# The remainders of the second feed-forward matrix formed by an adding DMA instead of VectorE, in a two-layer decoder trunk

## The chip, the cores and the metric

The kernel runs on one core of one Trainium2 chip. The metric is the device time of one execution in microseconds (us); lower is better.

## What is computed

The reference is a trunk of two layers on 512 tokens of width 1024, in float32. The first layer mixes with differential attention and block-sparse attention, the second with gated linear attention. Each mixer is followed by a residual, a layer norm, and a feed-forward network of 4096 hidden channels, and by another residual and norm. The change touches the feed-forward network alone:

```python
def sqrelu_mlp(x, w1, w2):
    return jnp.square(jax.nn.relu(x @ w1)) @ w2
...
x = layer_norm(DEEPNORM_ALPHA * x + mix, ln_mix_g[l], ln_mix_b[l])
x = layer_norm(DEEPNORM_ALPHA * x + sqrelu_mlp(x, ffn_w1[l], ffn_w2[l]), ln_ffn_g[l], ln_ffn_b[l])
```

## The kernel before, in words

**Split products.** Every large product is made in three passes. A float32 operand is split into a rounded part (type float32r) and a remainder, its difference from the rounded part, rounded in turn. `mm3` (L170 to L173) multiplies high by high, then the two mixed pairs. In the second feed-forward product the activations `hh` and `hl` are the stationary operands and the weights move: L171 takes the rounded part of the weight, L172 its remainder, L173 the rounded part again.

**The weight stream.** All weights lie in DRAM as units of 128x1024 float32 (512 KB), in the order in which they are used (`wst`). SP's queue loads them into a ring of four `raw` tiles (L92). `split_unit` (L114) pops one and calls `parts` (L105): ScalarE (ACT) copies it with rounding into half 0 of a `w` tile (L110), and VectorE (DVE) subtracts half 0 from `raw` and writes half 1 (L111). The `raw` tile is free again when both have read it. `w` tiles come from the pool `up` of eleven buffers; a count of slots (`W["cap"]`, 7 in the feed-forward network) limits how far ahead of their use units are split. `free` gives slots back when a unit has been used and calls `pump`, which splits the next unit.

**A feed-forward layer** (`ffn`) works in four blocks of eight hidden tiles (b = 0 to 3). In each block first the eight units of the first matrix are used, giving `hh` and `hl`, and then the eight units of the second matrix. In blocks 1 to 3 the first-matrix units are taken two at a time by `pair`, a scheme with seven products for eight, whose sums of weights `split_pair` forms on DVE (tile `sf`); block 0 uses six plain units and one pair. The products of the second matrix go to the four PSUM tiles `pf`, half a row of output at a time: four units for the first half, then four for the second. One such unit feeds 24 matmuls of 512 columns (2 slices of 128 channels, 4 token tiles, 3 passes). In the last block of each layer, POOL also loads the norm's gain and bias (`gb`, L290), by two DMAs on its own queue.

The order on each engine is set by the tile framework's scheduler, which may move an instruction ahead of others written earlier when its operands are ready. Each engine then works through its list in order.

Of the kernel before, what the change touches and what calls it, by code (L numbers as in the profile page):

```python
# [15 lines left out]
AF = mybir.ActivationFunctionType  # L16
ALU = mybir.AluOpType
AX = mybir.AxisListType

P = 128  # L20
# [4 lines left out]
FF = 4096  # L25
# [11 lines left out]
FBLK = 8  # L37
# [4 lines left out]
FFN_UNITS = (32, 128)  # L42
# [4 lines left out]
def trunk(ctx, tc, a, out):  # L47
    nc = tc.nc
    V, A, G, PE = nc.vector, nc.scalar, nc.gpsimd, nc.tensor
# [31 lines left out]
    wst = a["wst"]  # L81
# [2 lines left out]
    W = {"dma": 0, "split": 0, "used": 0, "slots": 0, "cap": 6}  # L84
    pairs = {u + 16 * b + j for u in FFN_UNITS for b in range(FF // P // FBLK) for j in range(0 if b else NPLAIN, FBLK, 2)}

    def dma_unit():
        for fn in late.pop(W["dma"], ()):
            fn()
        if W["dma"] < NU:  # L90
            r = rp.tile([P, 1024], F32, tag="raw", name="raw")
            nc.sync.dma_start(r, wst[W["dma"]])  # L92
            raws[W["dma"]] = r
            W["dma"] += 1

    def pop_raw():
        u = W["split"]
        while W["dma"] <= u:
            dma_unit()
        W["split"] += 1  # L100
        return raws.pop(u)

    def ahead():
        while W["dma"] < min(W["split"] + 4, NU):
            dma_unit()  # L105

    def parts(w, i, src):

        n = src.shape[-1] // 512
        A.activation(w[:, 0, i:i + n, :], src.rearrange("p (n c) -> p n c", n=n), AF.Copy)  # L110
        V.tensor_tensor(w[:, 1, i:i + n, :], src.rearrange("p (n c) -> p n c", n=n), w[:, 0, i:i + n, :].bitcast(F32),  # L111
                        op=ALU.subtract)

    def wtile():  # L114
        return up.tile([P, 2, 2, 512], F32R, tag="u", name="w")

    def split_unit():
        u = W["split"]
        if u in pairs:
            return split_pair(u)  # L120
        w = wtile()
        parts(w, 0, pop_raw())
        units[u] = w.rearrange("p s n c -> p s (n c)")
        W["slots"] += 1
        ahead()

    def split_pair(u):

        a1, a2 = pop_raw(), pop_raw()
        a11, a12, a21, a22 = a1[:, :512], a1[:, 512:], a2[:, :512], a2[:, 512:]  # L130
        ta, tb, tc_, td = (wtile() for _ in range(4))
        sf = t8("sf", (P, 2048))
        s1, s2, s3, s4 = (sf[:, 512 * i:512 * i + 512] for i in range(4))
        parts(ta, 0, a1)
        V.tensor_tensor(s1, a21, a22, op=ALU.add)
        V.tensor_tensor(s2, s1, a11, op=ALU.subtract)
        parts(tb, 0, sf[:, :1024])
        V.tensor_tensor(s3, a11, a21, op=ALU.subtract)
        V.tensor_tensor(s4, a12, s2, op=ALU.subtract)
        parts(tc_, 0, sf[:, 1024:])  # L140
        parts(td, 0, a22)
        units[u] = (ta, tb, tc_, td)
        W["slots"] += 4
        ahead()

    def pump():
        n = 4 if W["split"] in pairs else 1
        if W["split"] < NU and W["slots"] + n <= W["cap"]:
            split_unit()

    def nxt():
        u = W["used"]
        while W["split"] <= u:
            split_unit()
        W["used"] += 2 if u in pairs else 1
        return units.pop(u)
# [1040 lines left out]
```

## Time and profile before

| | us |
|---|---|
| median of three runs | 1173.81 |
| lowest and highest of them | 1173.73 and 1173.92 |
| the profiled execution, its own time | 1172.42 |
| its span, from first to last instruction | 1170.6 |

The profile is of one execution. It gives the busy time of each engine (PE is TensorE, PEld its weight loads), the chain of work that ended last, the waits between engines, and a timeline of instructions with start, duration and the idle time before each with what ended it. All times in it are counted from the start of the span.

### The profile page before, as it was taken

What the parts mean: (1) busy time and instruction counts of PE and PEld (TensorE: products, weight loads), DVE (VectorE), ACT (ScalarE), POOL (GpSimd) and SP (SyncE); (2) the same over time, 40 slices, a digit from 0 to 9 for tenths busy, and PEclk for the clock granted to TensorE, in tenths of its full rate; (3) what the DMA queues carried; (4) which work ended last, traced back from release to release, by engine and by line L of the source; (5) the groups of instructions that cost most, each with busy time, mean ns of one, the idle gap of its engine ahead of it and who ended that gap; (6) DMA issues with size and microseconds to landing.
All of it is one profiled execution on the core that took longest, in us unless ns stands there. A gap on an engine that the chain in (4) does not pass through costs nothing.

```text
span 1170.6 us, 16693 instructions
## 1 busy us (share of the span) xinstructions
PE 1155.2 (99%) x6682; PEld 1008.9 (86%) x6682; DVE 793.0 (68%) x1299; ACT 548.1 (47%) x890; POOL 48.4 (4%) x64
## 2 busy tenths in 40 slices
PE   9999999999999999999999999999999999999997
PEld 6788877898899899899888888888988998988986
DVE  6788673679468477487547656587784874865946
ACT  5745375547237146156236433643471551642631
POOL 1122300000000000000110000000000000000000
PEclk9999999999999999999999999999999999999999
DMA  9622050023226125127123122501051251251421
GB/s 319 232 72 73 8 161 32 19 73 118 99 60 191 38 73 180 54 67 252 37 68 108 55 72 73 180 19 57 34 181 54 70 165 55 87 165 36 121 78 73
DMA packets 34094, 114.33 MB, mean 98 GB/s; under 512 B 4192, under 2 KB 5216, under 8 KB 34016
## 3 DMA queue, kind: packets, MB, share of 16 engines
q1 hardware_dynamic: 32368, 108.22, 28.6%
q0 software_dynamic: 1648, 5.05, 1.4%
q8 instruction: 52, 0.85, 0.3%
q14 instruction: 26, 0.21, 0.1%
HBM read 111.15 MB, written 2.10 MB: 97 GB/s over the span
## 4 chain that ended last, share of the span: by engine, by line
PE 93%; issue 2%; ACT 2%; DVE 1%; DMA 0%; POOL 0%; DVEq 0%; ACTq 0%; POOLq 0%
PE pf L171 11%; PE pf L172 11%; PE pf L173 11%; PE pp L173 7%; PE pp L172 7%; PE pp L171 7%; PE pa L171 5%; PE pa L173 5%; PE pa L172 5%; PE pb L171 3%; PE pb L172 3%; PE pb L173 3%; PE pl L1000 2%; PE sc L521 1%; PE pv L171 1%
## 5 line engine op out<-in xcount | busy, mean ns | idle before, releaser
L111 DVE TENSOR_TENSOR w<-raw,w 128x1024 fp32r<-128x1024 f32 (+1 forms) x190 | 222.2, 1179 | 57.2 <-ACT w L110 56.3
L110 ACT ACTIVATE w<-raw 128x1024 fp32r<-128x1024 f32 (+1 forms) x190 | 188.2, 997 | 92.2 <-DMA raw<-in_wst 19.9
L171 PE MATMUL pf<-w,hh 128*128 128x512 f32 x504 | 196.4, 390 | 0.0
L172 PE MATMUL pf<-w,hh 128*128 128x512 f32 x504 | 196.2, 389 | 0.0
L173 PE MATMUL pf<-w,hl 128*128 128x512 f32 x504 | 196.1, 389 | 0.0
L110 ACT ACTIVATE w<-sf 128x1024 fp32r<-128x1024 f32 x52 | 55.0, 1058 | 215.6 <-PE pf L173 138.7
L172 PE MATMUL pp<-xTl,w 128*128 128x256 f32 x416 | 117.7, 283 | 0.0
L173 PE MATMUL pp<-xTh,w 128*128 128x256 f32 x416 | 117.7, 283 | 0.0
L171 PE MATMUL pp<-xTh,w 128*128 128x256 f32 x416 | 117.7, 283 | 0.0
L173 PEld LDWEIGHTS pf<-w,hl 128*128 128x128 f32 x504 | 94.6, 188 | 19.8
L171 PEld LDWEIGHTS pf<-w,hh 128*128 128x128 f32 x504 | 94.6, 188 | 19.5
L172 PEld LDWEIGHTS pf<-w,hh 128*128 128x128 f32 x504 | 94.6, 188 | 19.1
L171 PE MATMUL pa<-xTh,w 128*128 128x512 f32 x264 | 106.0, 403 | 0.0
L173 PE MATMUL pa<-xTh,w 128*128 128x512 f32 x264 | 103.1, 391 | 0.0
L172 PE MATMUL pa<-xTl,w 128*128 128x512 f32 x264 | 102.9, 390 | 0.0
L111 DVE TENSOR_TENSOR w<-sf,w 128x1024 fp32r<-128x1024 f32 x52 | 63.6, 1224 | 56.5 <-ACT w L110 56.5
L171 PE MATMUL pp<-T,w 128*128 128x256 f32 x312 | 88.3, 283 | 0.0
L172 PE MATMUL pp<-T,w 128*128 128x256 f32 x312 | 88.3, 283 | 0.0
L173 PE MATMUL pp<-T,w 128*128 128x256 f32 x312 | 88.3, 283 | 0.0
L171 PEld LDWEIGHTS pp<-xTh,w 128*128 128x128 f32 x416 | 79.8, 192 | 0.3
L172 PEld LDWEIGHTS pp<-xTl,w 128*128 128x128 f32 x416 | 79.8, 192 | 0.3
L173 PEld LDWEIGHTS pp<-xTh,w 128*128 128x128 f32 x416 | 79.8, 192 | 0.0
(260 smaller groups left out, 2264.2 us busy)
## 6 DMA issues: line engine op xcount, KB each, us to landing
raw<-in_wst SPq DMA_DIRECT2D x190, 512.0 KB, 3.8
xraw<-in_xT SPq DMA_DIRECT2D x8, 256.0 KB, 5.1
x<-in_x SPq DMA_DIRECT2D x4, 512.0 KB, 6.9
gb<-in_lng POOLq DMA_DIRECT2D x4, 512.0 KB, 5.7
gb<-in_lnb POOLq DMA_DIRECT2D x4, 512.0 KB, 7.5
out_x<-x SPq DMA_DIRECT2D x7, 256.0 KB, 2.0
tab<-in_rope SPq DMA_DIRECT2D x2, 512.0 KB, 5.9
raw<-in_wst SPq DMA_DIRECT2D x4, 128.0 KB, 4.4
```

The source lines that it names most:

```text
L110: A.activation(w[:, 0, i:i + n, :], src.rearrange("p (n c) -> p n c", n=n), AF.Copy)
L111: V.tensor_tensor(w[:, 1, i:i + n, :], src.rearrange("p (n c) -> p n c", n=n), w[:, 0, i:i + n, :].bitcast(F32), op=ALU.subtract)
L171: PE.matmul(o, l[0], r[0], start=first, stop=False)
L172: PE.matmul(o, l[0], r[1], start=False, stop=False)
L173: PE.matmul(o, l[1], r[0], start=False, stop=last)
L521: PE.matmul(ps[:, :n], q, k, start=i == 0, stop=False)
L1000: PE.matmul(pl[:, h * P:(h + 1) * P], z, z, start=True, stop=True)
```

## The change

For the 64 units of the second feed-forward matrix (eight in each of four blocks of two layers) DVE's subtraction is gone. ACT reads `raw` a second time and writes the negated rounded part into half 1 of the `w` tile. Then a DMA on POOL's queue reads the same unit again from DRAM and adds it to half 1. All other units, and the units of the first matrix, are split as before.

```diff
+    second = {u + 16 * b + 8 + j for u in FFN_UNITS for b in range(FF // P // FBLK) for j in range(FBLK)}
+
...
         w = wtile()
-        parts(w, 0, pop_raw())
+        raw = pop_raw()
+        if u in second:
+            A.activation(w[:, 0], raw.rearrange("p (n c) -> p n c", n=2), AF.Copy)
+            A.activation(w[:, 1], raw.rearrange("p (n c) -> p n c", n=2), AF.Copy, scale=-1.0)
+            nc.gpsimd.dma_start(w[:, 1], wst[u].rearrange("p (n c) -> p n c", n=2), accum_op=ALU.add)
+        else:
+            parts(w, 0, raw)
         units[u] = w.rearrange("p s n c -> p s (n c)")
```

In the changed kernel the lines behind the new code stand eight further down (`parts` is L112 and L113, the two new copies are L126 and L127, the DMA is L128, `p1` is L780). PE's list is the same in both, instruction for instruction.

ACT, block 0 of the first layer, from the last part of the pair's weights to the fifth second-matrix unit (`w_2627` is the block's first such unit; `r` and `hh` are the hidden activations, `p1` a partial sum of the pair). Before:

```order
L110 ACTIVATE w_2577<-raw_2443 128x512
L110 ACTIVATE w_2627<-raw_2479 128x1024
L707 ACTIVATE r_2657<-pa_2632 128x512
L110 ACTIVATE w_2664<-raw_2515 128x1024
L712 ACTIVATE r_2657<-r_2657 128x512
L110 ACTIVATE w_2704<-raw_2591 128x1024
L714 ACTIVATE hh_2660<-r_2657 128x512
L772 ACTIVATE p1_2675<-pp_2671 128x256
L110 ACTIVATE w_2736<-raw_2593 128x1024
L110 ACTIVATE w_2779<-raw_2630 128x1024
```

The same place in the changed kernel:

```order
L112 ACTIVATE w_2577<-raw_2443 128x512
L126 ACTIVATE w_2627<-raw_2479 128x1024
L127 ACTIVATE w_2627<-raw_2479 128x1024
L715 ACTIVATE r_2658<-pa_2633 128x512
L126 ACTIVATE w_2665<-raw_2515 128x1024
L720 ACTIVATE r_2658<-r_2658 128x512
L127 ACTIVATE w_2665<-raw_2515 128x1024
L722 ACTIVATE hh_2661<-r_2658 128x512
L126 ACTIVATE w_2706<-raw_2591 128x1024
L127 ACTIVATE w_2706<-raw_2591 128x1024
L780 ACTIVATE p1_2677<-pp_2673 128x256
L126 ACTIVATE w_2739<-raw_2593 128x1024
```

The second copy of the first unit stands right behind the first copy; the later units and `p1` stand one to three copies further back than they did.

POOL, last block of the first layer (`w_4973` is its first second-matrix unit). Before, these three stood next to each other:

```order
L290 DMA gb_5138<-in_lng 128x1024
L290 DMA gb_5138<-in_lnb 128x1024
L849 DMA wgr_5518<-in_wg 128x128
```

In the changed kernel:

```order
L128 DMA w_4973<-in_wst 128x1024
L128 DMA w_5017<-in_wst 128x1024
L128 DMA w_5070<-in_wst 128x1024
L298 DMA gb_5167<-in_lng 128x1024
L128 DMA w_5103<-in_wst 128x1024
L128 DMA w_5147<-in_wst 128x1024
L298 DMA gb_5167<-in_lnb 128x1024
L128 DMA w_5198<-in_wst 128x1024
L128 DMA w_5228<-in_wst 128x1024
L128 DMA w_5258<-in_wst 128x1024
L857 DMA wgr_5550<-in_wg 128x128
```

The block's eight adding DMAs stand around the two loads of `gb`; five of them come behind the first of these.

## Rows read from the trace of the kernel before

**Rows 1.** The page: span, busy time and share of each engine.
```profile
span 1170.6 us, 16693 instructions
PE 1155.2 (99%) x6682; PEld 1008.9 (86%) x6682; DVE 793.0 (68%) x1299; ACT 548.1 (47%) x890; POOL 48.4 (4%) x64
```

**Rows 2.** The page: the chain that ended last, shares of the span by engine.
```profile
PE 93%; issue 2%; ACT 2%; DVE 1%; DMA 0%; POOL 0%; DVEq 0%; ACTq 0%; POOLq 0%
```

**Rows 3.** PE's waits, all of 254 to 590 us, then all of 830 to 1162.
```profile
PE pf L171 <- ACT xTh L338: 0.3, 1, 0.3
...
PE pf L171 <- ACT xTh L338: 0.2, 1, 0.2
```

**Rows 4.** DVE's groups by line and form, 254 to 1170: idle before at the end.
```profile
L111 DVE TENSOR_TENSOR w<-raw,w 128x1024 fp32r<-128x1024 f32 x128 | 155.0, 1222 | 38.2 <-ACT w L110 37.7
```

**Rows 5.** Timeline of ACT: start, duration, instruction. Block 0, first unit and the pair's `hh`.
```profile
280.08 1.04 ACT L110 ACTIVATE w<-raw 128x1024 fp32r<-128x1024 f32 x1
281.03 0.58 ACT L707 ACTIVATE r<-pa 128x512 f32<-128x512 f32 x1
...
295.61 0.61 ACT L714 ACTIVATE hh<-r 128x512 fp32r<-128x512 f32 x1
```

**Rows 6.** Timeline of PE: the first unit's first uses, block 0, then the fourth unit's.
```profile
290.00 0.40 PE L171 MATMUL pf<-w,hh 128*128 128x512 f32 x1
290.24 0.40 PE L172 MATMUL pf<-w,hh 128*128 128x512 f32 x1
...
306.35 0.39 PE L171 MATMUL pf<-w,hh 128*128 128x512 f32 x1
```

**Rows 7.** Timeline, block 1: ACT's first copy, PE's first remainder, ACT's last `hh`.
```profile
359.66 1.06 ACT L110 ACTIVATE w<-raw 128x1024 fp32r<-128x1024 f32 x1 [0.35 <-PE pp L173]
360.63 0.37 ACT L772 ACTIVATE p<-pp 128x256 f32<-128x256 f32 x1
...
374.10 0.40 PE L172 MATMUL pf<-w,hh 128*128 128x512 f32 x1
...
377.40 1.14 ACT L714 ACTIVATE hh<-r 128x512 fp32r<-128x512 f32 x2
```

**Rows 8.** The page, DMA queues (packets, MB, share of 16 engines) and issues (median landing).
```profile
q1 hardware_dynamic: 32368, 108.22, 28.6%
q0 software_dynamic: 1648, 5.05, 1.4%
...
raw<-in_wst SPq DMA_DIRECT2D x190, 512.0 KB, 3.8
gb<-in_lng POOLq DMA_DIRECT2D x4, 512.0 KB, 5.7
gb<-in_lnb POOLq DMA_DIRECT2D x4, 512.0 KB, 7.5
```

**Rows 9.** Tile `gb`, landings of its two DMAs at 144, 536, 735 and 1113.
```profile
DMA to landing us min/median/max: 3.7/4.4/5.0
DMA to landing us min/median/max: 6.6/7.4/8.1
DMA to landing us min/median/max: 5.3/6.7/8.0
DMA to landing us min/median/max: 6.0/6.5/6.9
```

**Rows 10.** Busy time by stretch: PE, PEld, DVE, ACT, POOL, clock, DMA share, GB/s.
```profile
283.00:290.00 7.00, 7.00 (x60) 7.00 (x59) 6.60 (x10) 4.60 (x7) 0.00 (x0) 1.00 0.93 311
360.00:375.00 15.00, 15.00 (x122) 14.81 (x122) 14.27 (x22) 11.46 (x16) 0.00 (x0) 1.00 0.74 234
536.00:544.00 8.00, 8.00 (x59) 7.59 (x59) 7.73 (x12) 4.65 (x6) 1.04 (x2) 1.00 0.84 303
```

**Rows 11.** Timeline of POOL in the last block of the first layer.
```profile
536.28 0.53 POOL L290 DMA_DIRECT2D gb<-in_lng  x1 [390.94 <-PE pp L173]
```

**Rows 12.** Timeline of ACT, the last block's first second-matrix copy.
```profile
527.38 1.06 ACT L110 ACTIVATE w<-raw 128x1024 fp32r<-128x1024 f32 x1 [0.35 <-PE pp L173]
```

## The prediction, made before the changed kernel ran

> **What bounds the kernel.** I read the page's busy times first, then the chain, then PE's own waits in the two stretches of feed-forward work, and only then the engines that the change touches. PE is busy for 1155.2 of 1170.6 us [rows 1]; the reader is to see that 15.4 us is all that could be won without changing a matmul. The chain that ended last is PE for 93% and DVE for 1% [rows 2]. In the two feed-forward stretches PE waits once each for another engine, 0.3 and 0.2 us, both times for ACT's transposed input and never for a weight [rows 3]. So DVE, although it is busy for 793.0 us, is not what PE waits for here. What matters is the other question: how early each remainder is ready now, and whether the new path is still in time.
>
> **What goes from DVE.** The subtraction of 64 units, at 1222 ns each [rows 4]: 64 x 1.222 = 78.2 us, of 793.0. I cost the gain at nothing, since no PE wait in the stretch ends on DVE [rows 3]. Were all of PE's waits there gone, it would be 0.5 us.
>
> **What comes to ACT.** A second copy of the same shape for 64 units. A copy follows another at 281.03 - 280.08 = 0.95 us [rows 5], so 64 x 0.95 = 61 us on top of 548.1, on an engine that is 47% busy [rows 1]. What hides it is ACT's idle time, and behind that the lead of `hh`. In block 1 (and alike in 2 and 3) the last pair's `hh` end at 377.40 + 1.14 = 378.5 and the fourth unit uses them: 373.86 is where the first unit starts, 0.24 before its remainder at 374.10 [rows 7], and units follow at (306.35 - 290.00) / 3 = 5.45 us [rows 6], so that is 390.2. The lead is 11.7 us. ACT's new list puts twelve copies of second-matrix units ahead of this `hh` where eight stood: 4 x 0.95 = 3.8 us, still hidden if ACT's idle time (3.5 us of the 15 from 360 to 375 [rows 10]) took none of it. In block 0 the pair's `hh` ends at 296.2 and is used at 306.35 [rows 5, 6], a lead of 10.1 us. If that cover were gone, each further microsecond of ACT would be one of PE.
>
> **What comes to POOL and the DMA engines: the first unit.** After the second copy POOL issues a DMA of 512 KB, and PE's L172 waits for it. Its time is not in this trace; plain DMAs on the same queue and of the same size are. Below: the shortest of them, 3.7 us from issue to landing [rows 9]. Above: an addition has to read what is in SBUF as well as what is in DRAM, so it can move as much as two transfers. The nearest row for that is the second of the two `gb` loads, which lands when both are through: 5.0 to 8.1 us, median 7.5 [rows 8, 9]. In busy stretches even a first load took up to 6.6, and two more transfers' worth of engine time on top of it (1.70 each, below) make 10.0, my upper end. I take 7.5, because the DMA engines are 93% busy in the stretch that decides [rows 10], nearer to the rows at 536 than to those at 144.
>
> In block 0 the first unit's copy starts at 280.08; the second copy starts at 281.03 and ends at about 282.1 [rows 5]. The remainder is first read at 290.24 [rows 6], 8.1 us later. With 7.5 it lands at 289.6, 0.6 us early; with 3.7 it is 4.4 us early; with 8.1 it is just in time; with 10.0 it is 1.9 us late. The second layer's block 0 is built alike, so the upper end is 2 x 1.9 = 3.8 us. In blocks 1 to 3 the first copy ends at 360.7, `p` goes between, and the second ends at about 362.0 [rows 7]; the remainder is read at 374.10, 12.1 us later. All of 3.7 to 10.0 fits.
>
> **The later units.** PE takes one every 5.45 us, so a queue that delivers faster never falls behind. Plain transfers cost, in time of all 16 engines: 28.6% of 1170.6 us for 108.22 MB, or 1.62 us for one unit on SP's queue; 1.4% for 5.05 MB, or 1.70 us for one on POOL's [rows 8]. An adding transfer lies between 1.70 (one) and 3.40 (two). Beside it, while units are split in a burst, one `raw` load each has to pass: 3.3 to 5.0 us for both. Both ends are under 5.45, so the first unit is the only one that is tight, and I cost the others at nothing. The cover is 0.4 us per unit at the upper end, and more when the `raw` loads pause. The Trainium skill, "Collectives: The Full Stack", section "The bandwidth ceiling: the fold count and why AG ≠ RS ≠ AR", speaks against this change: a DMA that adds has two sources to read through one read ring and so moves data at half the rate of a copy. By that rule the transfer would cost an estimated 3.40 us and the sum would be the same, 0, with 0.4 us of cover per unit; at a copy's rate the cover would be 2.1 us. No run here shows yet which holds.
>
> **POOL's queue.** Issuing one DMA took 0.53 us [rows 11], eight in a block 4.2, against 43.6 us of matmuls for them (8 x 5.45). In the last block of a layer the loads of `gb` stand among them, and the first waited for PE until 536.28 [rows 11]; five adding DMAs now stand behind it, the fourth unit's first. That block's burst of copies begins at 527.38 [rows 12], so by block 1's distances (374.10 - 359.66 [rows 7], then 3 x 5.45) the fourth remainder is read at 558.2, 21.9 us after `gb` got its buffer. I cost this at nothing.
>
> **The sum.** 0 from DVE, 0 from ACT, 0 from the later units, 0 from the first unit with bounds 0 and 3.8. The profiled execution's own 1172.4 us stays 1172.4, and the runs' median, 1.4 us above it, stays **1173.8 us**.
>
> **The rivals.**
> - *Adding is dear in sustained rate (slower).* The place is the second matrix of all eight blocks, the point from which it decides 5.45 us of engine time for one adding transfer, 3.2 plain ones. At four plain ones (6.8 us) and even with no `raw` load beside them, the eighth of a block lands at 362.0 + 2 + 8 x 6.8 = 418.4 (2 us for what a landing of 3.7 holds beside 1.70 of transfer), and its use is 374.1 + 7 x 5.45 = 412.2: 6.2 us late, times 8 blocks 50 us, 1223 us; eight `raw` loads beside them, 8 x 1.62 = 13 us a block, could bring it to 1327. For it: no row shows an adding transfer or one that writes float32r. Against: plain transfers leave a factor of three. Chance 0.18.
> - *The first unit alone is late (a little slower).* Landings from 9.3 us on cost over 1.2 us in each layer, over 0.2% in all; 10.0 us gives 1177.6. For it: the busy DMA engines in that stretch [rows 10]. Against: the changed list frees `raw` tiles later for the second and third unit, so the loads beside it thin out. Chance 0.14.
> - *POOL cannot launch while DVE works (slower).* If DVE's instructions held back POOL's making of a DMA, the first unit of block 0 would be launched only in a gap of DVE, which is busy for 6.60 of the 7 us to 290 [rows 10]; launched then and landing 3.7 to 8.1 us later it is about 5 us late in each layer, 1184. The row against it: at 536.28 a DMA was issued in 0.53 us, and both landed by 8.1, in a stretch with DVE busy for 7.73 of 8 [rows 9 to 11]. The Trainium skill, "SBUF — State Buffer", has the rule in its note "The 'DVE blocks DMA' trap": DVE's two-port modes, such as a float32 copy, lock GpSimd out of writing descriptors. DVE's work here is tensor-tensor, for which the note does not claim that; the trace agrees as far as it goes. Chance 0.03.
> - *PE gains (faster).* DVE loses a tenth of its work, and anything that it held up would come earlier. PE's waits of 0.5 us are the ceiling: 1173.3, within the same. More would need faster matmuls, and the granted clock is already 1.00 of 2.4 GHz in every stretch shown [rows 10]. Chance 0.03.
>
> **How the numbers follow.** A measurement of this kernel can tell about 0.2% (2.35 us) from no change. No change to that bound: 0.62. Slower by more: 0.18 + 0.14 + 0.03 = 0.35. Faster by more: 0.03. The likeliest case alone runs from 1173.3 to 1176.2. The range reaches on to the cases of a late first unit and of a held launch, up to 1185; below, 1172.3 leaves room for a slight gain. Left out are the dear transfers, 0.18, and a real gain.
>
> **What would show it.** In the new profile PE's waits in 254 to 590 us should hold nothing for `w`, or only the L172 right behind the first L171 of block 0, around 290 and 867, by under 2 us. POOL's 64 DMAs should land in 5 to 10 us; DVE should be near 715 us, ACT near 609. The landings of one block should come closer together than 5.45 us. I am wrong if PE waits for `w` in blocks 1 to 3, with waits that grow from unit to unit: then the adding transfer is dear. I am also wrong if the landing is short and PE still waits: then ACT's second copy or POOL's queue is late.

## The result, and the profile after

The change makes the kernel slower: 1180.3 us median (1178.68 to 1181.48, four runs) against 1173.77, a ratio of 1.0055 with a 95% interval of 1.0038 to 1.0073. I had forecast 1173.8 us as the likeliest, with a chance of 0.35 for slower; the time lies inside the range but not in the case that I called likeliest.

The profiled execution took 1181.48 us. Its page, the lines that answer to [rows 1, 8]:

```profile
span 1179.7 us, 16801 instructions
...
PE 1159.7 (98%) x6682; PEld 1012.0 (86%) x6682; DVE 721.7 (61%) x1235; ACT 605.3 (51%) x954; POOL 104.2 (9%) x128
...
q1 hardware_dynamic: 32368, 108.22, 27.3%
q0 software_dynamic: 10864, 38.61, 15.8%
...
raw<-in_wst SPq DMA_DIRECT2D x190, 512.0 KB, 4.6
w<-in_wst POOLq DMA_DIRECT2D x64, 512.0 KB, 12.1
```

DVE lost 71.3 us and ACT gained 57.2, near the 78 and 61 that I had costed. The adding DMAs land in 12.1 us at the median, where I took 7.5 for the first of a block and had said 5 to 10 for all 64; by tile (`w` on POOL) their spread is

```profile
DMA to landing us min/median/max: 7.8/12.1/20.0
```

PE's waits in the same profile (in all, times, longest), all of them of 1 us or more and those of the feed-forward stretches:

```profile
PE pf L180 <- DMA w<-in_wst: 4.9, 4, 2.1
PE pn L601 <- ACT sh L596: 2.2, 1, 2.2
PE pt L536 <- ACT k L462: 1.8, 1, 1.8
PE idle L78 <- DVE zero L75: 1.2, 1, 1.2
PE p L179 <- ACT xTh L249: 1.1, 1, 1.1
PE pf L179 <- ACT xTh L346: 0.8, 3, 0.3
```

The first line is new. The reader is to see that 60 of 64 adding DMAs made PE wait for nothing, and four did. The timeline of PE shows which (start, duration, instruction, idle before and what ended it); L180 is the pass that reads the remainder:

```profile
293.80 0.50 PE L180 MATMUL pf<-w,hh 128*128 128x512 f32 x1 [1.98 <-DMA w<-in_wst]
...
570.49 0.50 PE L180 MATMUL pf<-w,hh 128*128 128x512 f32 x1 [0.31 <-DMA w<-in_wst]
...
574.28 0.50 PE L180 MATMUL pf<-w,hh 128*128 128x512 f32 x1 [2.14 <-DMA w<-in_wst]
575.54 0.60 PE L179 MATMUL pf<-w,hh 128*128 128x512 f32 x1
575.94 0.63 PE L180 MATMUL pf<-w,hh 128*128 128x512 f32 x1
...
578.93 0.43 PE L181 MATMUL pf<-w,hl 128*128 128x512 f32 x1
...
876.38 0.50 PE L180 MATMUL pf<-w,hh 128*128 128x512 f32 x1 [0.45 <-DMA w<-in_wst]
```

Two are the first unit of block 0, one in each layer (293.80 and 876.38). The other two are the seventh and eighth unit of the first layer's *last* block (570.49 and 574.28), a place where I had seen no danger. Behind the longest wait the matmuls take 0.63 us instead of 0.39. The table of stretches (PE, PEld, DVE, ACT, POOL, granted clock, DMA share, GB/s) shows the granted clock there, and at a place in the attention part:

```profile
176.00:180.00 4.00, 4.00 (x16) 3.47 (x16) 1.25 (x3) 3.07 (x7) 0.00 (x0) 0.57 0.50 161
...
576.00:579.00 3.00, 3.00 (x9) 2.35 (x8) 2.50 (x9) 1.74 (x4) 0.00 (x0) 0.50 0.00 0
579.00:582.00 3.00, 3.00 (x15) 2.47 (x14) 1.69 (x4) 0.00 (x0) 0.00 (x0) 1.00 0.00 0
```

From 576 to 579 the granted clock is 0.50, the lower level of 1.2 GHz; the eight steps from 575.54 to 578.93 take 3.39 us, where eight of 5.45 / 24 take 1.82, 1.6 us more. So the span's 9.1 us more are 4.9 us of waits for `w` and 4.5 us of longer busy time (1159.7 less 1155.2), with 0.3 us less of other idle time. Of the 4.5 us the stretch behind the last block's wait makes up 1.6, and the one at 176 us, which lies ahead of every adding DMA, an estimated 1.7 (4 us at 0.57). This execution was the slowest of the four; the median lies 1.2 us lower.

### The profile page after: what moved, and what is told of

Same layout as the page of the kernel before. It is cut to its first block, busy times and chain, and to the rows that moved or that the text cites. A ratio compares the mean times of both kernels' runs of the same rounds, so it can differ in the third digit from the quotient of the medians.

```text
span 1179.7 us, 16801 instructions
## 1 busy us (share of the span) xinstructions
PE 1159.7 (98%) x6682; PEld 1012.0 (86%) x6682; DVE 721.7 (61%) x1235; ACT 605.3 (51%) x954; POOL 104.2 (9%) x128
## 3 DMA queue, kind: packets, MB, share of 16 engines
q0 software_dynamic: 10864, 38.61, 15.8%
## 4 chain that ended last, share of the span: by engine, by line
PE 89%; DMA 4%; ACT 3%; issue 2%; DVE 1%; POOL 0%; SPq 0%; DVEq 0%; POOLq 0%; ACTq 0%
PE pf L180 11%; PE pf L179 10%; PE pf L181 10%; PE pp L181 6%; PE pp L180 6%; PE pp L179 6%; PE pa L179 5%; PE pa L181 5%; PE pa L180 5%; PE pb L179 4%; PE pb L180 4%; PE pb L181 4%; DMA w<-in_wst 3%; PE pl L1008 2%; PE sc L529 1%
## 5 line engine op out<-in xcount | busy, mean ns | idle before, releaser
L180 PE MATMUL pf<-w,hh 128*128 128x512 f32 x504 | 197.5, 392 | 4.9 <-DMA w<-in_wst 4.9
L113 DVE TENSOR_TENSOR w<-raw,w 128x1024 fp32r<-128x1024 f32 x126 | 144.9, 1156 | 76.3 <-ACT w L112 75.7
L112 ACT ACTIVATE w<-raw 128x1024 fp32r<-128x1024 f32 x126 | 120.7, 967 | 77.1 <-DMA raw<-in_wst 24.6
L112 ACT ACTIVATE w<-sf 128x1024 fp32r<-128x1024 f32 x52 | 55.0, 1058 | 176.6 <-PE pf L181 58.8
L128 POOL DMA_DIRECT2D w<-in_wst x64 | 55.9, 873 | 744.4 <-ACT w L127 724.5
L180 PE MATMUL pp<-xTl,w 128*128 128x256 f32 x416 | 117.8, 283 | 0.0
L180 PEld LDWEIGHTS pf<-w,hh 128*128 128x128 f32 x504 | 95.1, 189 | 25.7 <-DMA w<-in_wst 6.4
L180 PE MATMUL pa<-xTl,w 128*128 128x512 f32 x264 | 103.0, 390 | 0.0
L723 DVE TENSOR_TENSOR hl<-r,hh 128x512 fp32r<-128x512 f32 x64 | 44.2, 690 | 73.1 <-ACT hh L722 72.8
L180 PE MATMUL pp<-T,w 128*128 128x256 f32 x312 | 88.4, 283 | 0.0
L113 DVE TENSOR_TENSOR w<-sf,w 128x1024 fp32r<-128x1024 f32 x52 | 63.6, 1222 | 34.1 <-ACT w L112 34.1
L179 PEld LDWEIGHTS pp<-xTh,w 128*128 128x128 f32 x416 | 79.9, 192 | 0.3
## 6 DMA issues: line engine op xcount, KB each, us to landing
w<-in_wst POOLq DMA_DIRECT2D x64, 512.0 KB, 12.1
```

The source lines that it names most:

```text
L128: nc.gpsimd.dma_start(w[:, 1], wst[u].rearrange("p (n c) -> p n c", n=2), accum_op=ALU.add)
L179: PE.matmul(o, l[0], r[0], start=first, stop=False)
L180: PE.matmul(o, l[0], r[1], start=False, stop=False)
L723: V.tensor_tensor(l, r, h.bitcast(F32), op=ALU.subtract)
```

## The experiments

**Where the loss sits.** Theory A: only where an adding DMA is longer than the lead of its unit. Theory B: a small loss at each of the 64 units. Three kernels put the new path into parts of the network, a fourth takes it out at the late places:

```diff
-    second = {u + 16 * b + 8 + j for u in FFN_UNITS for b in range(FF // P // FBLK) for j in range(FBLK)}
+    second = {u + 16 * b + 8 + j for u in FFN_UNITS for b in (1, 2) for j in range(FBLK)}      # e1
+    second = {u + 8 + j for u in FFN_UNITS for j in range(FBLK)}                               # e2
+    second = {FFN_UNITS[0] + 48 + 8 + j for j in range(FBLK)}                                  # e3, e10
...
+    second -= {u + 8 for u in FFN_UNITS} | {FFN_UNITS[0] + 56 + j for j in range(4, FBLK)}     # e4, behind the line of the change
```

> The adding DMA only in blocks 1 and 2 of both layers (32 of 64 units); the other units are split on DVE as before. Theory A (late places): PE waits only for the first unit of block 0 and the last units of the last block, because only there an adding DMA of 8 to 20 us is longer than the lead; then this kernel has no PE wait for w and takes 1173.8 us within 0.2%. Theory B (every unit costs): the loss is spread over the units by the doubled DMA traffic and ACT's second copies, 6.5 us / 64 each; then it takes 1173.8 + 3.3 = 1177.0 us.

> The adding DMA only in block 0 of both layers (16 units). Theory A: PE waits for the first unit of block 0 as in the changed kernel, 2.1 us in the first layer and about 0.6 in the second, 1176.5 us, and up to 1.6 us more where a wait drops the granted clock. Theory B: 16 units, 1175.4 us, without a single long wait.

> The adding DMA only in the last block of the first layer (8 units). Theory A: the seventh and eighth unit are late as in the changed kernel, 2.6 us of waits and 1.6 us of lower clock behind them, 1176.4 to 1178.0 us. Theory B: 8 units, 1174.6 us.

> The whole change, but the late units stay on DVE: the first unit of block 0 in both layers and the last four units of the first layer's last block (6 of 64). Theory A: no PE wait for w is left, 1173.8 us within 0.2%. Theory B: 58 units still cost 5.9 us, 1179.7 us.

| kernel | units by DMA | median us | before, same chip | ratio, 95% interval | PE's waits for `w` in the profile |
|---|---|---|---|---|---|
| e1, blocks 1 and 2 | 32 | 1173.9 | 1173.12 | 1.0006 [0.9996, 1.0016] | none |
| e2, block 0 | 16 | 1175.99 | 1173.12 | 1.0017 [1.0006, 1.0028] | 1.9 us, 2 times |
| e3, last block, layer 1 of 2 | 8 | 1178.26 | 1173.12 | 1.0040 [1.0024, 1.0055] | 2.5 us, 2 times |
| e4, all but six | 58 | 1172.38 | 1173.12 | 0.9997 [0.9986, 1.0009] | none |

The ratio is worked out from all runs of both kernels, so it is not exactly the quotient of the two medians.

Theory B falls: 32 units cost nothing, 58 units cost nothing, and eight at the wrong place cost 0.4%. The losses of e2 and e3 add up to 0.57%, against 0.55% for the whole change. In e4 the 58 adding DMAs still take 11.8 us to land at the median; the page of e4 and PE's waits in its two feed-forward stretches read as those of before [rows 1, 3]:

```profile
PE 1155.8 (99%) x6682; PEld 1009.9 (86%) x6682; DVE 729.4 (62%) x1241; ACT 599.8 (51%) x948; POOL 99.3 (8%) x122
```
```profile
PE pf L180 <- ACT xTh L347: 0.3, 1, 0.3
...
PE pf L180 <- ACT xTh L347: 0.2, 1, 0.2
```

**What the parts cost by themselves.** e5 leaves the DMA out, e6 lets it copy instead of add:

```diff
-            nc.gpsimd.dma_start(w[:, 1], wst[u].rearrange("p (n c) -> p n c", n=2), accum_op=ALU.add)    # e5
+            nc.gpsimd.dma_start(w[:, 1], wst[u].rearrange("p (n c) -> p n c", n=2))                      # e6, in its place
```

> The DMA is left out: half 1 keeps the negated rounded part, so the remainders are not formed; DVE's 64 subtractions stay away and ACT's 64 second copies stay. Theory A: DVE's relief is worth nothing and ACT's copies are hidden, 1173.8 us within 0.2%. Rival (ACT's second copies cost): slower than before by more than 0.2%. Rival (DVE's relief gains): faster by more than 0.2%.

> The DMA copies the unit over half 1 instead of adding it (the remainders are replaced by the rounded weights); same queue, same size, same waits. Theory A (adding moves two operands): landings come 1.7 to 2.0 us apart in a burst instead of 3.8, the first lands in about 6 us instead of 8 to 10, PE waits for w nowhere, 1173.8 us within 0.2%. Rival (the cast to float32r or POOL's issue is what is slow): landings stay 3.8 us apart and 8 to 10 us for the first, 1178 to 1181 us.

e5: 1172.76 us against 1173.34, ratio 0.9996 [0.9987, 1.0005]. Taking away DVE's 64 subtractions and adding ACT's 64 copies changes nothing, as predicted. The run changes both at once; that neither counts by itself is argued from PE's waits, which in the feed-forward stretches of e5 hold only the 0.2 us for `xTh` in each layer, none for a split. e6: 1173.42 us, ratio 1.0000 [0.9991, 1.0009]; PE waits for `w` nowhere. Same queue, bytes and waits as in the change, so what is slow is the adding, not the cast to float32r or the second pass over DRAM. The lines of e6's page, its first DMA of block 0 (by tile `w` on POOL, mean and start, then the landing), and the same two lines of the changed kernel:

```profile
q0 software_dynamic: 10864, 38.61, 9.4%
...
w<-in_wst POOLq DMA_DIRECT2D x64, 512.0 KB, 7.3
...
L128 POOL DMA_DIRECT2D w<-in_wst x1: 530/530/530, 282.0 to 282.0; - x1
DMA to landing us min/median/max: 5.9/5.9/5.9
```
```profile
L128 POOL DMA_DIRECT2D w<-in_wst x1: 894/894/894, 283.8 to 283.8; - x1
DMA to landing us min/median/max: 9.9/9.9/9.9
```

With the 16.4 us of the other DMAs of this queue taken off [rows 8], one copy costs (9.4% x 1170.2 - 16.4) / 64 = 1.46 us of the 16 engines and one adding transfer (15.8% x 1179.7 - 16.4) / 64 = 2.66 us. POOL's instruction also lasts 0.87 us at the median for an adding DMA instead of 0.53. That landings in a burst come 1.7 to 2.0 us apart was not met: in block 0 they came 2.1 to 3.9 apart, where the `raw` loads share the engines (DMA share 1.06 from 285 to 305 us).

**The loads of `gb` in the last block.** POOL's order puts them between the adding DMAs. e7 moves them to SP's queue, e9 is e3 without them, e10 is e3 again on e9's chip:

```diff
-            nc.gpsimd.dma_start(gb[:, s, :], bass.AP(tensor=src.tensor, offset=src.offset + i * D, ap=[[0, P], [1, D]]))
+            nc.sync.dma_start(gb[:, s, :], bass.AP(tensor=src.tensor, offset=src.offset + i * D, ap=[[0, P], [1, D]]))    # e7, on the whole change
...
         gb = t8("gb", (P, 2, D))
+        if i == 1:                                                        # e9, on e3
+            V.memset(gb, 1.0)
+            return gb
```

> The whole change, with the loads of gb on SP's queue instead of POOL's. Theory A: in the first layer's last block the eighth unit lands earlier by the two loads that stood among the adding DMAs, about 5 us, and is in time; what stays is block 0, 2.7 us, 1176.5 us. Rival (the DMA engines, not the queue, are full there): the last block's wait stays, 1179 to 1181 us.

> As e3 (the adding DMA only in the last block of the first layer), but the two loads of gb for that layer are left out: DVE fills the tile with ones, so the norm's gain and bias are not applied there. Theory A1 (the two loads of 512 KB among the adding DMAs push the last units past their use): the eighth unit lands 5 to 7 us earlier and PE waits for no w in the last block; e3's 4.7 us go, 1173.3 us within 0.2%. Rival A2 (the order of use alone does it: the last four units are wanted 1.36 us apart there and land 3.8 us apart): waits of 2 us and more stay, 1176 us or more.

> e3 once more, for a second profile and beside e9 on one chip. Its waits for w in the profile were 2.5 us and its loss against before 4.7 us. Theory A: the rest is a lower clock, here behind the last block's waits or at 58 and 177 us, so the waits come again at 2.5 us and the time lies 3 to 5 us over before's. Rival: another wait, not for w, makes up the rest.

e9: 1174.09 us against 1174.08, ratio 1.0003 [0.9992, 1.0014], and no wait for a DMA. e10: 1178.08 us, 1.0031 [1.0019, 1.0043], with waits of 2.5 us at the two old places. The block's first adding DMA in POOL's timeline and the eighth unit's DMA, in e9, then in e10:

```profile
533.84 0.91 POOL L128 DMA_DIRECT2D w<-in_wst  x1 [386.00 <-ACT w L127]
...
L128 POOL DMA_DIRECT2D w<-in_wst x1: 872/872/872, 556.3 to 556.3; - x1
DMA to landing us min/median/max: 12.9/12.9/12.9
```
```profile
531.12 0.91 POOL L128 DMA_DIRECT2D w<-in_wst  x1 [386.20 <-ACT w L127]
...
L128 POOL DMA_DIRECT2D w<-in_wst x1: 866/866/866, 551.8 to 551.8; - x1
DMA to landing us min/median/max: 20.0/20.0/20.0
```

From issue to landing the eighth DMA is 7.1 us shorter in e9, but it is also issued later. Counted from the block's first adding DMA it lands 35.4 us on in e9 (556.3 + 12.9 - 533.84) and 40.7 in e10 (551.8 + 20.0 - 531.12), so the two loads ahead of it on the same queue are worth 5.3 us. In e9 PE first uses its remainder at 571.56, 2.4 us after it landed. So rival A2 (the order of use alone) falls. What the late units cost can be read from PE alone: from the block's first `pf` matmul to the first transposes behind it takes 32.67 us in before, e1, e4 and e9, 35.75 in e3 and 37.40 in e10, where the clock fell behind the wait. That is 3.1 and 4.7 us. The rest of what e3's profile lost against that of before lies ahead of the block (its first `pf` matmul starts at 544.28 instead of 541.58), where no adding DMA had been issued before 532 us and the clock was low at 58 and 176 us.

e7 missed: 1180.02 us, ratio 1.0047 [1.0034, 1.0060], instead of 1176.5. In its profile the last block's wait for `w` is gone, as expected: the eighth unit lands 35.7 us after the block's first adding DMA (529.87), as early as in e9, although both loads of `gb` are still made. So for the eighth unit it is their place on POOL's queue that counts, not their bytes. The eighth DMA in e7:

```profile
L128 POOL DMA_DIRECT2D w<-in_wst x1: 872/872/872, 555.4 to 555.4; - x1
DMA to landing us min/median/max: 10.2/10.2/10.2
```

A new wait stands in the old one's place, and block 0 makes PE wait 0.8 us instead of the 2.7 expected. PE's waits in e7, then DVE's timeline:

```profile
PE pt L343 <- DVE x L335: 2.6, 1, 2.6
...
PE pf L180 <- DMA w<-in_wst: 0.8, 2, 0.4
```
```profile
558.03 1.23 DVE L113 TENSOR_TENSOR w<-raw,w 128x1024 fp32r<-128x1024 f32 x1 [9.57 <-ACT w L112]
565.63 1.22 DVE L113 TENSOR_TENSOR w<-raw,w 128x1024 fp32r<-128x1024 f32 x1 [6.37 <-ACT w L112]
567.62 2.47 DVE L113 TENSOR_TENSOR w<-raw,w 128x1024 fp32r<-128x1024 f32 x2 [0.77 <-ACT w L112]
570.01 0.68 DVE L306 SCALAR_TENSOR_TENSOR x<-x,pf 128x512 f32<-128x512 f32 x1
```

On SP's queue the loads of `gb` hold up the `raw` loads behind them (one issued at 543.7 took 20.8 us to land; the slowest of this block in e10 took 12.9); ACT waits for `raw`, DVE for ACT, and DVE's additions to the residual (L306) stand behind those splits in its list, so the norm and PE's transposes come late. The wait moved from PE's weights to PE's transposes. The profile is that of the fastest of e7's five runs (1175.99 us, near what was expected); what made the other four 3 to 4 us longer is not in it and stays open.

No run was made for the second layer's last block, but the trace of the changed kernel shows why it was spared. POOL's order there is the same, with both loads of `gb` among the adding DMAs, and PE takes the last four units in the same quick order. But SP issues the last of all `raw` loads at 1125.0. From 1136.4 on an adding DMA lands 2.5 us behind the DMA ahead of it, and the second load of `gb` 1.2 us; in the first layer, beside the `raw` loads of the next weights, it was up to 3.9 and 2.6 us. The eighth unit lands at 1147.6, 6.3 us before PE reads its remainder (its DMA, then PE's timeline):

```profile
L128 POOL DMA_DIRECT2D w<-in_wst x1: 863/863/863, 1136.6 to 1136.6; - x1
DMA to landing us min/median/max: 11.0/11.0/11.0
...
1153.95 0.39 PE L180 MATMUL pf<-w,hh 128*128 128x512 f32 x1
```

**Once more.**

> The changed kernel itself once more, for a second profile. Theory A: waits for w at the same four places, 5 us in all; the lower clock at 176 us, which lies ahead of any adding DMA, need not come again, and the span is then 1.5 us shorter. If it comes again at the same place, the change has to do with it.

1178.57 us, ratio 1.0048 [1.0035, 1.0060]. The four waits came at the same places, 4.2 us in all; behind none of them did the clock fall this time, and the place at 176 us had its lower clock again, which the expectation had named as a sign against the change. But e1, e2, e3, e9 and e10 have it too, and e10 issues no adding DMA before 531 us; the profiles of before, e4, e5, e6 and e7 have it not. The stretch in e10, with the one behind e10's last wait under it, and then in before:

```profile
176.00:179.50 3.50, 3.50 (x15) 2.89 (x15) 0.92 (x2) 2.85 (x7) 0.00 (x0) 0.53 0.55 166
571.00:575.00 4.00, 3.22 (x8) 2.57 (x9) 0.91 (x4) 0.00 (x1) 0.00 (x0) 0.65 0.34 140
```
```profile
176.00:179.50 3.50, 3.50 (x20) 2.56 (x20) 1.22 (x3) 3.16 (x7) 0.00 (x0) 1.00 0.67 211
```

The place stands behind a wait of PE of 2.2 us that is none of the change's; in before it is

```profile
PE pn L593 <- ACT sh L588: 2.2, 1, 2.2
```

At 58 us, behind another wait (`pt` for `k`), one program goes both ways: from 58 to 61 us the clock is 1.00 in the first profile of the change (wait 1.8 us) and 0.53 in e8 (2.2), 1.00 in e10 (2.0) and 0.50 in e3 (2.4); e5 keeps 1.00 behind 2.4. The runs of before spread as well (1171.52 to 1176.64 us in 29), and their mean granted clock with them: 0.997 to 0.999 in the ten fastest, 0.994 to 0.996 in the seven slowest. So it is not the adding DMAs' doing. What decides it in an execution is not shown.

## Why the prediction was wrong, point by point

**What bounds the kernel: right.** Freeing DVE, with ACT's copies in its place, gains nothing (e5), and the question was whether each remainder is in time.

**ACT's second copies: right.** 57 us more on ACT, hidden (e5). In block 0 the first unit's second copy started 282.47 - 281.53 = 0.94 us behind the first, as costed; ACT's timeline in the changed kernel:

```profile
281.53 1.04 ACT L126 ACTIVATE w<-raw 128x1024 fp32r<-128x1024 f32 x1
282.47 1.05 ACT L127 ACTIVATE w<-raw 128x1024 fp32r<-128x1024 f32 x1
```

**The first unit of block 0: mechanism right, size off.** I took 7.5 us for the landing, with bounds of 3.7 and 10.0 and a lead of 8.1 us. It measured 9.9 us in the first layer, near the upper bound, and 8.4 in the second, and made PE wait 1.98 and 0.45 us. In the three other profiles with this unit the two waits were 1.46 and 0.23 (e8), 1.61 and 0.29 (e2), 0.39 and 0.45 (e7). e2 puts the whole of it at 0.17%. A term of 0 with bounds 0 and 3.8 should have been 0.8 to 2.4.

**POOL's queue, "I cost this at nothing": the step that failed.** I asked whether the fourth unit of the last block would still be in time behind the wait of `gb` for its buffer, and it was: it landed at 556.5, and PE read it at 561.86. I did not ask for the eighth. Two things were left out. The loads of `gb` are themselves transfers of 512 KB on the queue ahead of the last units, and put off the eighth landing by 5.3 us (e9 against e10). And I used 5.45 us between units for all eight, where the second half of that block takes all four units for one token tile before the next (the loop for `fin and half == 1` in `ffn`), so that they are wanted one quarter of 5.45, 1.36 us, apart. The order of POOL showed the one, the code the other. In the first layer it took both to make PE wait: without the loads the earlier use does no harm (e9), and in the usual order of use the eighth unit would be wanted 3 x (5.45 - 1.36) = 12.3 us later, where it was 2.1 us late; this second half is worked out from the trace and was not run. The same 5.45 stands under "The later units", so "the first unit is the only one that is tight" fell with it. The term of 0 measured 2.4 to 2.5 us of waits and 3.1 to 4.7 us of PE's time in the block; by the runs' times it is 0.40% in e3 and 0.31% in e10, more than half of the whole.

**The later units elsewhere: right.** Blocks 1 and 2 cost nothing (e1). I had bounded an adding transfer with the `raw` load beside it by 3.3 and 5.0 us; in the burst of block 0 the stretch of the changed kernel is full (the DMA share is 1.01, where it was 0.45 before):

```profile
285.00:320.00 35.00, 33.02 (x172) 28.22 (x171) 12.95 (x20) 20.33 (x26) 6.10 (x7) 1.00 1.01 266
```
```profile
285.00:320.00 35.00, 35.00 (x177) 29.83 (x176) 21.37 (x28) 13.20 (x16) 0.00 (x0) 1.00 0.45 150
```

In it the block's eight adding DMAs landed 3.4 to 3.9 us apart, under PE's 5.45 and inside my bounds. In the last two units of the last block that made PE wait, the ends of the waits are 574.28 - 570.49 = 3.8 us apart, the same pace. What I had said of the landings missed all the same: not 5 to 10 us but up to 20.0, since a burst is issued faster than it lands: in the first layer's last block the time from issue to landing grows from 9.0 us for the first unit to 20.0 for the eighth. The Trainium skill's rule, given for reduce-scatter in a ring, that a DMA that adds runs at half the rate of a copy ("Collectives: The Full Stack", section "The bandwidth ceiling: the fold count and why AG ≠ RS ≠ AR") is nearly met: 2.66 against 1.46 us of engine time is a factor of 1.8, and the landings at the end of the second layer, 2.5 against 1.2 us apart, make it 2.1.

**The rivals.** The dear transfer did not come, since 2.66 us is far from 5.45. POOL held back by DVE did not come: the first adding DMA was issued about 0.3 us behind its copy's end (283.8 behind 282.47 + 1.05). DVE was idle at that moment (from 283.4 on), but block 1's first was issued at 365.94, as soon behind its copy, while DVE was busy from 365.40 to 366.08. The late first unit came, at 2.4 us. By itself it is worth e2's 0.17%, about the 0.2% that parts slower from same; what took the time well over it is the last block, which none of them named.

**The clock was no step of mine.** Behind the last block's wait the granted clock fell to 0.50 for some 3 us in the profile of the change and to 0.65 of a 4 us stretch in e10's, and not in e3's and e8's. It was worth some 1.6 us in each of the two (PE's time in the block: 37.34 against 35.78 us in the two profiles of the change, 37.40 against 35.75 in e10 and e3).

No version beat the kernel before. With the late six units left on DVE (e4) the two are equal, because PE does the same matmuls without a pause in both.

## What to carry to other kernels

Moving work from an engine that nobody waited for gained nothing here, although it was busy for 68% of the span; what can come of it is a longer path, so list the lead of every consumer, not of the first one or of a typical block. Where a loop takes its operands in another order at the end, or the queue that you add to has other transfers in between, that place needs a line of its own in the sum. A run that took six of the 64 units out of the change lost nothing, and that one run told a loss at a few places from a loss at every unit.

## What the runs showed of the hardware

- Adding during a DMA cost the DMA engines 2.66 us per 512 KB where a copy on the same queue cost 1.46 (e6). POOL's instruction for it lasted 0.87 us where a copy's lasted 0.53; a load queued right behind one started 0.53 us after it in the changed kernel (540.58 behind 540.05) and 0.83 us in e10, so how long it holds POOL up is not settled.
- An adding DMA of 512 KB landed in 7.3 us at best (e7), against 3.7 for the quickest plain load on this queue [rows 9]; behind others in a burst it took up to 20.1 (e8).
- Adding DMAs on one queue landed 3.4 to 3.9 us apart in the burst of block 0, beside `raw` loads, and 2.5 us apart at the end of the second layer, where there were none.
- A wait of some 2 us on PE was followed by a stretch at the lower clock in some executions and not in others, with the same program and the same wait (2.14 us in the changed kernel's two profiles: 0.50 behind it in one, 1.00 in the other).
